# A two-block model on one core: router slots from a threshold, conditioning blocks moved into the conformer, and five smaller edits

## The chip, the cores and the metric

One core of a Trainium2 chip runs the whole forward pass in one launch. The metric is the device time of one execution in microseconds; lower is better. TensorE does the matmuls (PE in the profile, its weight loads PEld), VectorE is DVE, ScalarE ACT, GpSimd POOL, SyncE SP. SP, ACT and POOL also issue DMAs.

## The reference

The input is 512 tokens of width 1024 in float32. A first block mixes tokens (an RWKV-7 mixer in both directions beside a gated linear attention, GLA) and then runs a mixture of 32 experts. A second block has two layers: layer 0 mixes with RG-LRU and Hyena filters, layer 1 with a conformer convolution, and after each stands a mixture of 16 experts in which every expert picks its tokens:

```python
def _adaln(cvec, w_mod, b_mod, n_chunks):
    m = jax.nn.silu(cvec) @ w_mod[:, :n_chunks * D_MODEL] + b_mod[:n_chunks * D_MODEL]
    return [m[:, None, j * D_MODEL:(j + 1) * D_MODEL] for j in range(n_chunks)]

def _ec_moe(h, router, w1, w3, w2):
    cap = EC_CAPACITY * n // N_EXPERTS_2                     # 64 tokens for each expert
    probs = jax.nn.softmax(jnp.einsum('bnd,de->ben', h, router).astype(jnp.float32), axis=1)
    gates, idx = lax.top_k(probs, cap)
    xs = h[bidx, idx]
    a = jnp.einsum('becd,edf->becf', xs, w1)
    g = jnp.einsum('becd,edf->becf', xs, w3)
    y = jnp.einsum('becf,efd->becd', jax.nn.silu(a) * g, w2) * gates[..., None].astype(h.dtype)
    return jnp.zeros_like(h).at[bidx, idx].add(y)

# each layer l of the second block, x of 512 tokens
sh1, sc1, g1, sh2, sc2, g2 = _adaln(c, w_mod[l], b_mod[l], N_MOD)    # N_MOD = 6
xl = xl + g1 * mixer(_modulate(_rmsnorm(xl, norm1_g[l]), sh1, sc1))
xl = xl + g2 * _ec_moe(_modulate(_rmsnorm(xl, norm2_g[l]), sh2, sc2), ...)
```

The kernel takes the softmax over the experts for each token, and the order of tokens within an expert doesn't matter to the sum.

## The kernel before

The program is one stream of instructions for each engine. A framework takes the Python program, gives tiles their memory and lets its scheduler order the instructions of every engine by its own estimate of their times, earlier lines of the program first where several are ready; on the chip each engine then follows its fixed order and waits where something is late. A tile with `bufs=n` rotates over n buffers.

`phase1` (L238) normalises the input (L305 to L316: squares, one root for the four token tiles, a scaling by ScalarE, transposes into `hT`), runs four `rwkv_pair`s and the GLA, and fills in twelve conditioning blocks: `adaln_block(l, j)` (L899) streams 8 tiles of 512 KB of `w_mod` through two buffers and multiplies them by the conditioning vector, four column groups at a time (L905, L907); j = 0, 1, 3, 4 give shifts and scales in `mods`, j = 2 and 5 give gates that go through memory. `mixed` (L616) writes the mixer's output by a DMA on SP.

`residual` (L787) multiplies by the output projection, and `norm_tile` (L857) transposes each token tile, multiplies it by the router, takes the root of the mean square and writes the normalised rows to `xrow`. `moe1` (L1518) runs 16 pairs of the first 32 experts; the output rows of the first 15 go to memory (`yslot`) and are gathered back for each token (L1672, L1673), those of the last pair are added by a matmul (L1690) with a gate matrix `ohT` that is made before it (L1675 to L1683).

`moe2` (L1838) is the experts of the second block. From the router's logits it makes the softmax (L1871 to L1876), transposes it to 16 experts by 512 tokens, finds the 64th largest value of each expert by eight rounds of MAX8 (L1886, L1888), then counts and scans along the tokens to number the slots (L1891 to L1899) and transposes back to `R` (L1902, L1904). `experts` (L1774) prepares each pair of experts: a one-hot matrix `oh` (L1783, for two pairs at a time), a matmul that reads token indices from it (L1789), a gather of the rows (L1711), transposes to `xT` (L1716) and a transposed one-hot `ohT` (L1798). `ffn` does up and gate (L1493) and down (L1513) from a ring of weight tiles of 1 MB (`ring`, L1447), and `outputs` scales and adds (L1750 to L1761).

`mixer1` (L1345) is the conformer: for each of eight feature tiles two products (`product`, L1199, 24 matmuls each, weights split into two parts by ScalarE and VectorE), then 14 convolution taps on VectorE (L1378) and running sums; after the loop the statistics (L1363).

Of the kernel before, what the change touches and what calls it, by code (L numbers as in the profile page):

```python
# [20 lines left out]
T, D = 512, 1024  # L21
NT, KT = 4, 8
# [157 lines left out]
class Kern:  # L180
# [57 lines left out]
    def phase1(self, _):  # L238
# [4 lines left out]
        with ExitStack() as es:  # L243
# [61 lines left out]
            for t in range(NT):  # L305
                nc.scalar.activation(S("bk", D), xs[t], AF.Square, accum_out=rs[:, t:t + 1])
            nc.scalar.activation(rs, rs, AF.Sqrt, scale=1.0 / D, bias=self.eps)
            V.reciprocal(rs, rs)
            for t in range(NT):
                nc.scalar.activation(xs[t], xs[t], AF.Copy, scale=rs[:, t:t + 1])  # L310
                for b in range(2):
                    ps = bank("mm").rearrange("p (a b) -> p a b", a=4)
                    for k in range(4):
                        nc.tensor.transpose(ps[:, k], xs[t][:, (4 * b + k) * 128:(4 * b + k + 1) * 128], ident)
                    V.tensor_mul(hT[:, 4 * b:4 * b + 4, 128 * t:128 * t + 128], ps,
                                 c("ln1_w", 4 * b, 4)[:, :, None].to_broadcast([128, 4, 128]))  # L316
# [9 lines left out]
            def shifted(ft, out):  # L326
# [16 lines left out]
                     for l in range(2) for j in range(6))  # L343
# [5 lines left out]
            fill(6)  # L349
# [5 lines left out]
            fill(3)  # L355
            gl(99)
            fill(99)
# [499 lines left out]
    def norm_tile(self, M, W, bank, t, wr, ps_):  # L857
        nc, V = self.nc, self.nc.vector
        x = self.xres[:, t]
        xn = M.xn[t]  # L860
        rs = M.rs[:, t:t + 1]
        xT = W([128, KT, 128], "xTt", bufs=2)
        for b in range(2):
            ps = bank(("gat", "cb")[b], 1).rearrange("p (k n) -> p k n", k=4)
            for k in range(4):
                nc.tensor.transpose(ps[:, k], x[:, 512 * b + 128 * k:512 * b + 128 * k + 128], self.ident)
            (V.tensor_copy if b else nc.scalar.copy)(xT[:, 4 * b:4 * b + 4], ps)
        for k in range(KT):
# [476 lines left out]
    def mixer1(self, ey):  # L1345
# [3 lines left out]
        with ExitStack() as es:  # L1349
# [8 lines left out]
            us, acc = [], []  # L1358

# [6 lines left out]
            for i in range(KT):  # L1366
# [151 lines left out]
    def moe1(self, yT):  # L1518
        nc, tc, A = self.nc, self.tc, self.A
        with ExitStack() as es:  # L1520
# [138 lines left out]
            for pair in range(15):  # L1659
                if pair % 2 == 0 and pair < 14:  # L1660
                    tokens(pair // 2 + 1)
                z = slice(128 * pair, 128 * pair + 128)
                xT = self.rows_load(P, bank, tok[:, pair:pair + 1], 128) if pair else xT0
                self.rows_ffn(P, bank, xT, self.yslot[z], self.take, 2)
# [3 lines left out]
            for t in range(NT):  # L1668
                for j, g in enumerate((w1, e2)):
# [4 lines left out]

            oh = P([128, D], "yo", bufs=2)[:, 0:512].rearrange("p (t e s) -> p t e s", t=NT, e=2)  # L1675
            V.tensor_tensor(oh, R[:, :, 30:32, None].to_broadcast([128, NT, 2, 64]),
                            self.iota[:, None, None, 0:64].to_broadcast([128, NT, 2, 64]), op=OP.is_equal)
            V.tensor_mul(oh, oh, gl[:, :, :, None].to_broadcast([128, NT, 2, 64]))
            ps = bank("tr", 1)
            for t in range(NT):  # L1680
                nc.tensor.transpose(ps[:, 128 * t:128 * t + 128], oh[:, t].rearrange("p e s -> p (e s)"), self.ident)
            ohT = P([128, KT, 128], "xT", bufs=2).rearrange("p k n -> p (k n)")[:, 0:T]
            nc.scalar.copy(ohT, ps)  # L1683
# [52 lines left out]
    def outputs(self, P, bank, ys, g, m, g2, ohT, last=False):  # L1736
# [5 lines left out]
        def parts(n):  # L1742
            a, b = (P([128, 512], t, F32R, bufs=2 if last and n else self.nbuf)
                    for t in (("h", "h") if last and n and self.nbuf == 1 else ("yhi", "ylo")))
# [3 lines left out]
            else:  # L1748
                y = P([128, 512], "y32")
# [24 lines left out]
    def experts(self, P, bank, R, gt, affine, ne, ff, g2):  # L1774
# [4 lines left out]
        def prepare(pair):  # L1779

            if pair % 2 == 0:
                oh = self.oh = P([128, NT, 4, 64], "oh", F32R)
                V.tensor_tensor(oh, R[:, :, 2 * pair:2 * pair + 4, None].to_broadcast([128, NT, 4, 64]),  # L1783
                                self.iota[:, None, None, 0:64].to_broadcast([128, NT, 4, 64]), op=OP.is_equal)
            oh = self.oh[:, :, 2 * (pair % 2):2 * (pair % 2) + 2]
# [52 lines left out]
    def moe2(self, l, yT):  # L1838
        nc, tc, A, V = self.nc, self.tc, self.A, self.nc.vector
        with ExitStack() as es:  # L1840
# [24 lines left out]
            self.ring_more(M, (ring, "w", 7 + l, 7 + l))  # L1865
# [15 lines left out]
            q, wk, gt, eq = (P([128, T], n, **k)[:16] for n, k in (("hT", dict(bufs=2)), ("y32", {}), ("h", dict(bufs=2)), ("h", dict(bufs=2))))  # L1881
            nc.scalar.copy(q, ps[:16])
            V.tensor_copy(wk, q)
            m8 = P([16, 8], "m8")
            for r in range(8):
                V.max(out=m8, in_=wk)  # L1886
                if r < 7:
                    V.match_replace(out=wk, in_to_replace=m8, in_values=wk, imm_value=-1.0)  # L1888
            cnt = P([16, 1], "c16")
            one = self.ones[:16, 0:1].to_broadcast([16, T])  # L1890
            V.tensor_scalar(gt, q, m8[:, 7:8], 0.0, op0=OP.is_gt, op1=OP.add, accum_out=cnt)  # L1891
            V.tensor_scalar(cnt, cnt, -1.0, 64.0, op0=OP.mult, op1=OP.add)
            V.tensor_scalar(eq, q, m8[:, 7:8], None, op0=OP.is_equal)
            V.tensor_tensor_scan(wk, one, eq, 0.0, OP.mult, OP.add)
            V.scalar_tensor_tensor(eq, wk, cnt, eq, op0=OP.is_le, op1=OP.mult)
            V.tensor_add(gt, gt, eq)
            V.tensor_tensor_scan(wk, one, gt, 0.0, OP.mult, OP.add)
            V.tensor_mul(wk, wk, gt)
            V.tensor_scalar(wk, wk, -1.0, None, op0=OP.add)  # L1899
            ps = bank("tr", 1)[:, 0:64].rearrange("p (t n) -> p t n", t=NT)  # L1900
            for t in range(NT):
                nc.tensor.matmul(ps[:, t], wk[:, 128 * t:128 * t + 128], self.ident[:16, 0:16], start=True, stop=True)  # L1902
            R = P([128, NT, 16], "R")
            V.tensor_copy(R, ps)  # L1904
# [3 lines left out]
            V.scalar_tensor_tensor(gt[:, :, :, 0], R, 0.0, p, op0=OP.is_ge, op1=OP.mult)  # L1908
# [120 lines left out]
```

## Time and profile before

| | us |
|---|---|
| median of 3 runs (lowest, highest) | 2886.4 (2882.2, 2889.4) |
| the profiled execution | 2891.0 |
| its span, first to last instruction | 2889.4 |
| TensorE busy in the span | 2454.6 |
| VectorE busy | 1124.1 |
| ScalarE busy | 643.5 |
| moved by DMA | 778.4 MB, mean 269 GB/s |

Times in the trace are microseconds from the span's start. The stages follow each other: `phase1` to 606, the first experts to 1303, the mixer of layer 0 to 1560, its residual to 1606, its experts to 2136, the conformer to 2288, its residual to 2346, the last experts to 2870, the final norm to 2889. A matmul of float32 shows as two instructions, a transpose as one.

### The profile page before, as it was taken

The page shows a single profiled execution, that of the slowest core. Times are in us where ns is not written, and L with a number is a line of the kernel's source. Part 1 is how long each engine was busy: PE and PEld are TensorE (multiplying, and loading weights), DVE is VectorE, ACT ScalarE, POOL GpSimd, SP SyncE. Part 2 cuts the span into 40 slices and gives each one's busy share as a digit, 9 for nine tenths or more (in the row PEclk, how much of TensorE's full clock was granted, in tenths as well). Part 3 has the DMA queues.
Part 4 walks back from the last instruction along what each step waited for, and adds up shares of the span by engine and source line. Part 5 has one row for each costly group of instructions (what it writes and reads, how often), then busy time and mean ns, then how long its engine had stood idle before and what let it go on. Part 6 is the DMA issues. An engine that isn't in the chain of part 4 may idle for free. (4 is left out here: it accounts for less than half of the span.)

```text
span 2889.4 us, 36529 instructions
## 1 busy us (share of the span) xinstructions
PE 2454.6 (85%) x15158; PEld 1352.8 (47%) x15158; DVE 1124.1 (39%) x2143; ACT 643.5 (22%) x1049; POOL 107.0 (4%) x193
## 2 busy tenths in 40 slices
PE   7999998775999988868889688988989669888897
PEld 3565655663534544436567433333347553333343
DVE  3867767534121320015875411111239641211112
ACT  3223313221102430005721200010034321000001
POOL 1000000001110000010000000000000000000000
PEclk9999998776999999988899798999999779999999
DMA  4355343056998999983133599999954259999996
GB/s 150 121 174 171 108 129 124 18 187 251 396 367 328 397 393 398 396 346 124 59 124 135 208 409 386 392 406 405 409 195 132 104 203 362 399 405 405 400 409 252
DMA packets 244551, 778.42 MB, mean 269 GB/s; under 512 B 15963, under 2 KB 17243, under 8 KB 243488
## 3 DMA queue, kind: packets, MB, share of 16 engines
q1 hardware_dynamic: 223616, 711.77, 65.2%
q0 software_dynamic: 12448, 41.50, 3.7%
q10 hardware_dynamic: 8320, 22.80, 2.2%
q8 instruction: 120, 1.97, 0.3%
q14 instruction: 47, 0.39, 0.0%
HBM read 748.73 MB, written 27.28 MB: 269 GB/s over the span
## 5 line engine op out<-in xcount | busy, mean ns | idle before, releaser
L1493 PE MATMUL G<-w,xT 128*64 128x256 f32 (+1 forms) x4096 | 772.4, 507 | 22.5 <-DMA w<-in_moe_w_up_dram 18.1
L1493 PEld LDWEIGHTS G<-w,xT 128*64 128x64 f32 x4096 | 293.1, 140 | 380.2 <-issue 287.6
L1513 PE MATMUL Y<-w,hT 128*64 128x512 f32 x1536 | 402.7, 602 | 2.6 <-DMA w<-in_moe_w_down_dram 1.3
L1513 PEld LDWEIGHTS Y<-w,hT 128*64 128x64 f32 x1536 | 172.2, 137 | 195.3 <-issue 182.6
L1498 DVE TENSOR_TENSOR h<-h,G 128x256 f32<-128x256 f32 (+1 forms) x64 | 35.4, 553 | 516.8 <-PE G L1493 406.8
L1761 DVE TENSOR_TENSOR xres<-xres,cb 128x512 f32<-128x512 f32 x116 | 79.6, 687 | 115.4 <-PE cb L1759 115.4
L1750 DVE SCALAR_TENSOR_TENSOR y<-Y,gate,g 128x512 f32<-128x512 f32 x32 | 24.0, 751 | 233.9 <-PE Y L1513 232.3
L321 PE MATMUL mm<-hT,w 128*128 128x512 f32 x240 | 113.2, 611 | 0.0
L1716 PE MATMUL gat<-ident,xg 128*128 128x128 f32 x128 | 30.4, 371 | 95.4 <-DMA xg<-xrow,tok 95.3
L1497 ACT ACTIVATE h<-G 128x256 f32<-128x256 f32 (+1 forms) x64 | 31.4, 491 | 343.3 <-PE G L1493 337.6
L1504 ACT COPY hT<-tr 128x256 f32<-128x256 f32 (+1 forms) x64 | 30.7, 479 | 274.8 <-PE tr L1503 274.8
L907 PE MATMUL ad<-wm,sc 128*32 128x256 f32 x768 | 70.5, 410 | 20.5 <-DMA wm<-in_w_mod_dram 19.1
L1209 PE MATMUL b<-big,wh 128*128 128x512 f32 x320 | 84.2, 415 | 4.4 <-ACT wh L854 3.0
L1751 ACT CAST yhi<-y 128x512 fp32r<-128x512 f32 x30 | 18.6, 619 | 310.5 <-DVE y L1750 224.2
L1716 PEld LDWEIGHTS gat<-ident,xg 128*128 128x128 f32 x128 | 19.1, 183 | 117.9 <-DMA xg<-xrow,tok 88.2
L1209 PEld LDWEIGHTS b<-big,wh 128*128 128x128 f32 x320 | 63.0, 199 | 22.6 <-ACT big L1190 5.4
L1759 PEld LDWEIGHTS cb<-yhi,ohT 128*128 128x128 f32 x114 | 21.4, 188 | 105.2 <-DVE xres L1761 56.8
L1503 PE MATMUL tr<-ident,h 128*128 128x128 f32 x192 | 35.8, 297 | 39.1 <-DVE h L1498 39.0
L636 PE MATMUL g<-wb,hT 128*64 128x128 f32 x1024 | 65.5, 276 | 3.3 <-DVE ga L711 2.6
L321 PEld LDWEIGHTS mm<-hT,w 128*128 128x128 f32 x240 | 42.9, 190 | 51.3 <-issue 50.3
L1759 PE MATMUL cb<-yhi,ohT 128*128 128x512 f32 x114 | 57.5, 504 | 9.7 <-ACT yhi L1751 9.7
L1711 POOL DMA_INDIRECT xg<-xrow,tok x32 | 31.1, 972 | 887.6 <-DVE tok L1793 435.7
(677 smaller groups left out, 3564.7 us busy)
## 6 DMA issues: line engine op xcount, KB each, us to landing
w<-in_exp_w_dram SPq DMA_DIRECT2D x384, 1024.0 KB, 13.2
w<-in_moe_w_gate_dram SPq DMA_DIRECT2D x64, 1024.0 KB, 15.6
w<-in_moe_w_up_dram SPq DMA_DIRECT2D x64, 1024.0 KB, 15.0
w<-in_moe_w_down_dram SPq DMA_DIRECT2D x64, 1024.0 KB, 15.3
wm<-in_w_mod_dram SPq DMA_DIRECT2D x96, 512.0 KB, 4.2
ws<-in_w_in_dram SPq DMA_DIRECT2D x20, 512.0 KB, 4.1
ws<-in_cf_w_dram SPq DMA_DIRECT2D x20, 512.0 KB, 3.5
st<-in_w_out_dram SPq DMA_DIRECT2D x16, 512.0 KB, 4.1
```

The lines of the kernel that those rows point to most:

```text
L321: nc.tensor.matmul(ps[:m], w[:, k, col0:col0 + m], hT[:, k], start=k == 0, stop=k == KT - 1)
L636: nc.tensor.matmul(ps[half[h], b], hT[:, k, 64 * j:64 * j + 64], w[h][:, k], start=k == 0, stop=k == KT - 1)
L907: nc.tensor.matmul(ps[32 * g:32 * g + 32, 0:256], self.sc[:, k], w[:, 256 * g:256 * g + 256], start=k == 0, stop=k == KT - 1, tile_positio ...
L1209: nc.tensor.matmul(ps, a[:, k], b[:, k], start=m == 0 and k == 0, stop=m == 2 and k == KT - 1)
L1493: nc.tensor.matmul(parts[m][64 * c:64 * c + 64], xT[:, k, 64 * e:64 * e + 64], w[:, kk, H * c:H * c + H], start=k == 0, stop=k == KT - 1)
L1497: nc.scalar.activation(h, parts[0], AF.Silu)
L1498: nc.vector.tensor_mul(h, h, parts[1])
L1503: nc.tensor.transpose(ps[:, j].rearrange("p c s -> p (c s)"), h[:, 128 * j:128 * j + 128], self.ident)
L1513: nc.tensor.matmul(ys[n][64 * e:64 * e + 64], hTs[e][:, f], ws[e][:, ff_, 512 * n:512 * n + 512], start=f == 0, stop=f == nf - 1)
L1716: nc.tensor.transpose(ps[:, k], xg[:, 512 * b + 128 * k:512 * b + 128 * k + 128], self.ident[:m, :m])
L1759: nc.tensor.matmul(ps, ohT[:m, 128 * t:128 * t + 128], p[k][:m], start=k == 0, stop=k == 1)
L1761: V.tensor_add(xr, xr, ps)
```

## The change

- **Norm of phase 1**: the root is taken for each token tile alone; instead of scaling the tile on ScalarE, VectorE makes a diagonal matrix `dg` of the scales (one buffer), and the transposes become matmuls with it.
- **Conditioning**: `phase1` does eight of the twelve blocks, (0, 0) to (0, 5), (1, 0) and (1, 1). The conformer does (1, 2) to (1, 5), one behind each of its feature tiles 1 to 4, with two buffers for `w_mod` tiles, and sets up the conditioning vector anew.
- **`mixed`** issues its DMA on ScalarE's queue.
- **`norm_tile`**: the root goes to a tile `sd` of its own; for the last token tile an Exp of it, whose result nobody reads, follows.
- **Gate matrix of the first experts**: `ohT` is made during pair 2, in the buffer that held `lnrow`.
- **Later experts**: MAX8 reads the transposed softmax from PSUM; the 64th value goes back to all partitions by a matmul, tokens above and equal to it are counted by matmuls in bf16, and the slots follow by operations with tokens on the partitions. `oh` is made for each pair alone. Some buffers change places, and the ring has one tile more (18 in both layers instead of 17).

```diff
-            nc.scalar.activation(rs, rs, AF.Sqrt, scale=1.0 / D, bias=self.eps)
-            V.reciprocal(rs, rs)
-            for t in range(NT):
-                nc.scalar.activation(xs[t], xs[t], AF.Copy, scale=rs[:, t:t + 1])
+                r = rs[:, t:t + 1]
+                nc.scalar.activation(S("bk", D), xs[t], AF.Square, accum_out=r)
+                nc.scalar.activation(r, r, AF.Sqrt, scale=1.0 / D, bias=self.eps)
+                V.reciprocal(r, r)
+                dg = P([128, 128], "nwr")
+                V.tensor_scalar(dg, ident, r, None, op0=OP.mult)
...
-                        nc.tensor.transpose(ps[:, k], xs[t][:, (4 * b + k) * 128:(4 * b + k + 1) * 128], ident)
+                        nc.tensor.matmul(ps[:, k], xs[t][:, (4 * b + k) * 128:(4 * b + k + 1) * 128], dg, start=True, stop=True)
...
-                     for l in range(2) for j in range(6))
+                     for l, j in ((0, 0), (0, 1), (0, 2), (0, 3), (0, 4), (0, 5), (1, 0), (1, 1)))
...
-            fill(6)
+            fill(4)
...
-            fill(3)
+            fill(2)
             gl(99)
-            fill(99)
...
-        self.nc.sync.dma_start(self.ymix[k], o)
+        self.nc.scalar.dma_start(self.ymix[k], o)
...
-        nc.scalar.activation(rs, rs, AF.Sqrt, scale=1.0 / D, bias=self.eps)
-        V.reciprocal(rs, rs)
+        sd = M.P([128, 2], "sd")
+        nc.scalar.activation(sd[:, 0:1], rs, AF.Sqrt, scale=1.0 / D, bias=self.eps)
+        V.reciprocal(rs, sd[:, 0:1])
+        if t == NT - 1:
+            nc.scalar.activation(sd[:, 1:2], sd[:, 0:1], AF.Exp)
...
+            self.adaln_setup(P)
...
+                if 0 < i < 5:
+                    self.adaln_block(1, i + 1, lambda: H([128, D], "junk", bufs=2), bank, lambda: P([128, T], "t2", bufs=4)[:, 0:256])
...
+                if pair == 2:
+                    lnrow = M.P([128, D], "lnrow")
+                    oh = lnrow[:, 0:512].rearrange("p (t e s) -> p t e s", t=NT, e=2)
...
+                    ohT = lnrow[:, 512:1024]
+                    nc.scalar.copy(ohT, ps)
...
-            self.ring_more(M, (ring, "w", 7 + l, 7 + l))
+            self.ring_more(M, (ring, "w", 8 + l, 8 + l))
...
+            dg, ps = P([16, 16], "dg"), bank("bg", 1)[:, 0:16]
+            V.tensor_scalar(dg, self.ident[:16, 0:16], m8[:, 7:8], None, op0=OP.mult)
+            nc.tensor.matmul(ps, self.ones[:16], dg, start=True, stop=True)
+            th = P([128, 16], "th")
+            V.tensor_copy(th, ps)
+            m = P([128, NT, 2, 16], "gq", BF16)
+            t3 = th[:, None].to_broadcast([128, NT, 16])
+            V.tensor_tensor(m[:, :, 0], p, t3, op=OP.is_gt)
+            V.tensor_tensor(m[:, :, 1], p, t3, op=OP.is_equal)
+            ps = bank("tr", 1)[:, 0:160].rearrange("p (t a n) -> p t a n", t=5, a=2)
+            for t in (4, 0, 1, 2, 3):
+                for s_ in range(t):
+                    nc.tensor.matmul(ps[:, t], self.onesb, m[:, s_], start=s_ == 0, stop=t == 4 and s_ == 3)
+                if t < 4:
+                    nc.tensor.matmul(ps[:, t], self.beforeb, m[:, t], start=t == 0, stop=True)
+            need, pos = P([128, 16], "need"), ps[:, 0:4]
+            V.tensor_scalar(need, ps[:, 4, 0], -1.0, 64.0, op0=OP.mult, op1=OP.add)
+            n3 = need[:, None].to_broadcast([128, NT, 16])
+            R, eq = P([128, NT, 16], "R"), P([128, NT, 16], "eq")
+            V.tensor_tensor(eq, pos[:, :, 1], n3, op=OP.is_lt)
+            V.tensor_mul(eq, eq, m[:, :, 1])
+            V.tensor_add(eq, eq, m[:, :, 0])
+            V.tensor_tensor(R, pos[:, :, 1], n3, op=OP.min)
+            V.tensor_add(R, R, pos[:, :, 0])
+            V.scalar_tensor_tensor(R, R, 1.0, eq, op0=OP.add, op1=OP.mult)
+            V.tensor_scalar(R, R, -1.0, None, op0=OP.add)
```

## Rows read from the trace of the kernel before

**Rows 1.** Stretches: us, each engine's busy us (instructions), TensorE clock, DMA share, GB/s.
```profile
40.00:480.00 440.00, 414.75 (x4643) 257.59 (x4643) 311.58 (x622) 132.04 (x224) 14.60 (x30) 0.97 0.41 132
480.00:606.00 126.00, 87.89 (x1312) 71.80 (x1308) 66.16 (x163) 32.25 (x51) 1.95 (x4) 0.74 0.14 48
...
1649.00:2136.00 487.00, 439.04 (x1887) 173.30 (x1886) 84.17 (x147) 44.77 (x90) 5.68 (x6) 0.95 0.97 384
...
2161.00:2223.00 62.00, 61.82 (x273) 51.19 (x274) 53.07 (x90) 24.75 (x29) 0.00 (x0) 1.00 0.31 98
```
**Rows 2.** Waits, 1649 to 2140 (TensorE), 1560 to 2121 (SP's queue): total, times, longest.
```profile
PE gat L1716 <- DMA xg<-xrow,tok: 27.8, 6, 5.7
...
SPq L1447 <- PE G L1493: 294.7, 114, 30.7
```
**Rows 3.** Timeline in phase 1: start, duration, engine, operation, [idle before, releaser].
```profile
198.60 0.64 PE L907 MATMUL ad<-wm,sc 128*32 128x256 f32 x8 [0.77 <-DMA wm<-in_w_mod_dram]
```
**Rows 4.** The tile wm: who waited for it, us in total, times.
```profile
  PE ad L907: 19.1, 19
```
**Rows 5.** Stretch 40 to 480, instructions of line 907 alone.
```profile
40.00:480.00 440.00, 59.03 (x672) 16.01 (x672) 0.97 0.41 132
```
**Rows 6.** Timeline of the conformer, TensorE and VectorE.
```profile
2228.67 3.78 PE L1209 MATMUL b<-hh,wh 128*128 128x512 f32 x8 [5.08 <-ACT wh L854]
...
2267.86 3.57 PE L1363 MATMUL s<-ones,sum 128*128 128x1 f32 x16 [14.43 <-DVE sum L1388]
...
2259.83 7.25 DVE L1378 SCALAR_TENSOR_TENSOR cy<-ug,pc,cy 128x64 f32<-128x64 f32 x14 [1.44 <-ACT cy L1374]
```
**Rows 7.** Timeline of the router of layer 0, up to the gathered rows.
```profile
1612.94 1.28 ACT L1873 ACT_TABLE_LOAD   x1
...
1617.21 0.57 ACT L1882 COPY hT<-tr 16x512 f32<-16x512 f32 x1 [2.72 <-PE tr L1880]
...
1618.27 0.68 DVE L1886 MAX8 m<-y 16x8 f32<-16x512 f32 x1
...
1629.43 0.73 DVE L1891 TENSOR_SCALAR_CACHE_REDUCE h<-hT,m 16x512 f32<-16x512 f32 x1
...
1638.01 0.25 DVE L1908 SCALAR_TENSOR_TENSOR gt<-R,prob 128x64 f32<-128x64 f32 x1
1638.15 1.22 DVE L1783 TENSOR_TENSOR oh<-R,iota 128x1024 fp32r<-128x1024 f32 x1
...
1642.04 1.01 POOL L1711 DMA_INDIRECT xg<-xrow,tok  x1 [28.29 <-DVE tok L1793]
...
1646.77 1.12 PE L1716 MATMUL gat<-ident,xg 128*128 128x128 f32 x4 [0.62 <-DMA xg<-xrow,tok]
```
**Rows 8.** Timeline of the first router: its counts in bf16.
```profile
682.04 0.27 PE L1598 MATMUL gat<-ab,onesb 128*128 128x32 bf16 x4
```
**Rows 9.** The chain that ended last, a gather late in the last layer: start, us.
```profile
2715.96 8.27 DMA xg<-xrow,tok
```
**Rows 10.** Timeline of the first experts' end, TensorE and ScalarE's queue.
```profile
1288.09 1.09 PE L1681 MATMUL tr<-ident,yo 128*128 128x128 f32 x4 [11.38 <-DVE yo L1678]
...
1295.63 7.67 PE L1513 MATMUL Y<-w,hT 128*64 128x512 f32 x32
...
1303.33 0.36 ACTq L1213 DMA_DIRECT2D eo<-in_ln_f_w_dram  x1
```
**Rows 11.** The tile w, 1255 to 1320: issues (ns min/median/max, first and last start), landings.
```profile
L1447 SPq DMA_DIRECT2D w<-in_moe_w_down_dram x4: 2473/3393/3702, 1261.0 to 1270.8; - x4
...
DMA to landing us min/median/max: 21.8/22.5/22.8
```
**Rows 12.** Timelines in phase 1: scaling, transposes, two-pass matmuls of 128x128.
```profile
15.94 4.27 ACT L310 ACTIVATE ar<-ar,rs 128x1024 f32<-128x1024 f32 x4 [0.24 <-DVE rs L308]
...
23.88 1.10 PE L314 MATMUL mm<-ident,ar 128*128 128x128 f32 x8
...
207.44 1.16 PE L462 MATMUL sc<-ident,bk 128*128 128x128 f32 x8
```

More of the change, by code (lines that the diff above doesn't have):

```diff
@@ L305, in phase1 @@
             for t in range(NT):
-                nc.scalar.activation(S("bk", D), xs[t], AF.Square, accum_out=rs[:, t:t + 1])
-            nc.scalar.activation(rs, rs, AF.Sqrt, scale=1.0 / D, bias=self.eps)
-            V.reciprocal(rs, rs)
-            for t in range(NT):
-                nc.scalar.activation(xs[t], xs[t], AF.Copy, scale=rs[:, t:t + 1])
+                r = rs[:, t:t + 1]
[4 more added lines that the diff above has]
+                V.tensor_scalar(dg, ident, r, None, op0=OP.mult)
                 for b in range(2):
@@ L1661, in moe1 @@
                     tokens(pair // 2 + 1)
+                if pair == 2:
+                    lnrow = M.P([128, D], "lnrow")
+                    oh = lnrow[:, 0:512].rearrange("p (t e s) -> p t e s", t=NT, e=2)
+                    V.tensor_tensor(oh, R[:, :, 30:32, None].to_broadcast([128, NT, 2, 64]),
+                                    self.iota[:, None, None, 0:64].to_broadcast([128, NT, 2, 64]), op=OP.is_equal)
+                    V.tensor_mul(oh, oh, gl[:, :, :, None].to_broadcast([128, NT, 2, 64]))
+                    ps = bank("tr", 1)
+                    for t in range(NT):
+                        nc.tensor.transpose(ps[:, 128 * t:128 * t + 128], oh[:, t].rearrange("p e s -> p (e s)"), self.ident)
+                    ohT = lnrow[:, 512:1024]
+                    nc.scalar.copy(ohT, ps)
                 z = slice(128 * pair, 128 * pair + 128)
@@ L1673, in moe1 @@
                     V.scalar_tensor_tensor(self.xres[:, t], y, g[:, t:t + 1], self.xres[:, t], op0=OP.mult, op1=OP.add)
[L1675 to L1683, printed above, removed]
             o = self.rows_ffn(P, bank, xT, None, self.take, 2)
@@ L1743, in parts @@
             a, b = (P([128, 512], t, F32R, bufs=2 if last and n else self.nbuf)
-                    for t in (("h", "h") if last and n and self.nbuf == 1 else ("yhi", "ylo")))
+                    for t in (("hT", "hT") if last and n and self.nbuf == 1 else ("yhi", "ylo")))
             if g2 is None:
@@ L1748, in parts @@
             else:
-                y = P([128, 512], "y32")
+                y = P([128, 512], "h", bufs=2)
                 V.scalar_tensor_tensor(y[:m], ys[n][:m], g[:m], g2[:m, 512 * n:512 * n + 512], op0=OP.mult, op1=OP.mult)
@@ L1779, in prepare @@
         def prepare(pair):
[L1781 to L1785, printed above, removed]
+            oh = P([128, NT, 2, 64], "oh", F32R)
+            V.tensor_tensor(oh, R[:, :, 2 * pair:2 * pair + 2, None].to_broadcast([128, NT, 2, 64]),
+                            self.iota[:, None, None, 0:64].to_broadcast([128, NT, 2, 64]), op=OP.is_equal)
             ps = bank("bg", 1)
@@ L1880, in moe2 @@
                 nc.tensor.matmul(ps[:16, 128 * t:128 * t + 128], p[:, t], self.ident, start=True, stop=True)
[L1881 to L1884, printed above, removed]
+            wk, m8 = P([128, T], "hT", bufs=2)[:16], P([16, 8], "m8")
             for r in range(8):
-                V.max(out=m8, in_=wk)
+                q = wk if r else ps[:16]
+                V.max(out=m8, in_=q)
@@ L1887, in moe2 @@
                 if r < 7:
[L1888 to L1902, printed above, removed]
@@ L1903, in moe2 @@
-            R = P([128, NT, 16], "R")
-            V.tensor_copy(R, ps)
+                    V.match_replace(out=wk, in_to_replace=m8, in_values=q, imm_value=-1.0)
+            dg, ps = P([16, 16], "dg"), bank("bg", 1)[:, 0:16]
[4 more added lines that the diff above has]
+            m = P([128, NT, 2, 16], "gq", BF16)
@@ L1906, in moe2 @@
+            V.scalar_tensor_tensor(R, R, 1.0, eq, op0=OP.add, op1=OP.mult)
+            V.tensor_scalar(R, R, -1.0, None, op0=OP.add)
             gt = P([128, NT, 16, 3], "gt")
             V.tensor_copy(gt[:, :, :, 1:3], self.tokid[:, :, None].to_broadcast([128, NT, 16, 2]))
-            V.scalar_tensor_tensor(gt[:, :, :, 0], R, 0.0, p, op0=OP.is_ge, op1=OP.mult)
+            V.tensor_mul(gt[:, :, :, 0], p, eq)
             self.experts(P, bank, R, gt, affine, 16, 1024, g2)
```

## The prediction

> **What bounds the kernel now.** I read the stages first, then who waits in each, then the rows around every edit. The profiled execution took 2891.0 us (span 2889.4 and 1.6 around it), 4.6 above the median of 2886.4 of the runs; the sum below is made on the profile and then taken off the median.
>
> By stages [rows 1]: in the first mixer, from 40 to 480, TensorE is busy 414.75 of 440 us, VectorE 311.58. So TensorE's throughput sets the pace there; the tail from 480 to 606 is a chain of short steps (TensorE 87.89 of 126 at a clock of 0.74). In the first expert layer of the second block (1649 to 2136) TensorE is busy 439.04 of 487, and DMA carries 384 GB/s. Both look full, so the waits decide: TensorE's longest wait in that stretch is for gathered rows (27.8 us in six), no wait for a weight is listed at all, and it is the loads' queue that waits for TensorE to free slots, 294.7 us [rows 2]. Weights are not late; TensorE is the bound, and what counts is when its first matmul can start. The other expert layer of that block repeats this. In the conformer's product loop (2161 to 2223) TensorE is busy 61.82 of 62 us and VectorE 53.07 [rows 1]: TensorE is full, VectorE close behind.
>
> **Part by part.** *Adaln blocks out of phase 1.* One weight tile of a block costs TensorE 8 matmuls in 0.64 us, a block of 8 tiles 5.1, four blocks 20.5 [rows 3]. Waits for w_mod tiles cost 19.1 us over twelve blocks, so four carry 6.4 more: 26.9 us at most [rows 4]. Of the 12 x 64 matmuls 672 lie between 40 and 480 [rows 5]; the other 96, 1.5 blocks, lie before that or in the tail, where TensorE has gaps, and I count them at nothing. That leaves 2.5 blocks of 6.7, or 16.8 us, of throughput. A sixth of it I give back, since with less matmul work the mixer's own chains will show their waits: -14, bounds -27 and 0. The 32 w_mod loads go from SP too, and with them what they held up there.
>
> *The same four blocks in the conformer.* They sit between products in a loop where TensorE is full. They bring 20.5 us of matmuls and, at phase 1's mean, 6.4 of waits. Hidden are three things [rows 6]. TensorE stands 5.08 us for a weight tile at 2228.67. After that pause it runs at the lower clock (8 matmuls in 3.78 us, the usual time being nearer 2): about 3 us. And it waits 14.43 us for the sums at 2267.86, while VectorE's last slice needs 7.25 for its taps and, as I estimate it, some 3.5 around them: 3.5 us of slack. 26.9 - 5.1 - 3 - 3.5 gives +15. Behind the waiting matmuls stand the next products on TensorE, and behind the w_mod loads, which wait for one of two buffers, the product weights on SP. If each tile waits as in the densest stretch of phase 1 (0.77 us at 198.60 [rows 3], on half of the 32 tiles, 12 us) and nothing is hidden, it is 20.5 + 12, or +33; if the blocks fall into the pauses, +3.
>
> *Slots of the later experts* (twice). Up to the one-hot matrix `oh`, the chain of the router loses three things [rows 7]. The Exp table load ahead of the softmax (1.28) moves to where ScalarE idles. The two copies before the first MAX8 go, from 1617.21 to 1618.27 (1.06). And the scans: from 1629.43 to the end of `oh` (1638.15 + 1.22) are 9.94 us. In their place come a tiny matmul with an operation before and one after it, some 0.8 us; two comparisons and eight operations on at most 128x64, 0.25 each as L1908, 2.5; 14 bf16 count matmuls, where four took 0.27 [rows 8], under 1; half of `oh`, 0.6; and hand-overs, about 0.5. That is 5.4, so 4.5 less. Together the token index is 6.8 us earlier. What is late next is the gather: issued at 1642.04, it was used at 1646.77, 4.7 us later [rows 7]; 6.8 us earlier it runs beside weight loads, as the gather that took 8.27 [rows 9]. So the first expert matmul comes 3.3 to 6.8 earlier; I take 5.5, since the ring is nearly filled by then. Twice: -11, bounds -7 and -14.
>
> *One more weight buffer.* Nothing waits for weights [rows 2]: 0. Were DMA the bound, one load of 1.05 MB at 384 GB/s would be worth 2.7 us in each layer, -5; a fuller queue could lengthen the gathers, whose mean wait is 4.6 us in six cases: at most +2.
>
> *Gate matrix early.* At the end of the first experts, TensorE stands 11.38 us at 1288.09 behind the transposes of `oh`, for VectorE; the last pair's matmuls are queued behind them, and its Y ends 7.67 us after 1295.63 [rows 10]. With `oh` long done, the last w_down tile is late next: issued up to 1270.8, landing 22.5 us on, at 1293.3 [rows 11]. The quarter of Y that needs it ends near 1297 to 1300: 3 to 6 us earlier. But the matrix now lies in the `lnrow` buffer until the last add, some 7 us past Y, and the next mixer's first buffer `eo` starts its load at 1303.33, right when Y ends, so it seems to wait for that memory. If it must now wait for the adds, nothing is left, or +3. I take -1, bounds -5 and +3. The early work (two operations, four transposes, one copy) hides under pair 2.
>
> *Norm at the start.* Four scalings by ScalarE (4.27 us [rows 12]) go; 32 transposes become matmuls with a diagonal. Eight transposes took 1.10 us, four two-pass matmuls of that size 1.16 [rows 12], so each tile pays about 1.1 more, and the one diagonal buffer makes tiles wait for each other. Tile 0 starts earlier, the last tile hardly: -1, bounds -4 and +3. The Trainium skill ("TensorE: Matmul & The Clock Gate", Terms) says that the transpose mode is four times faster for FP32; by that factor the 32 matmuls would cost about 13 us more instead of 4, which no row bears out, as the two-pass form stands at twice.
>
> *The output of the mixer on ScalarE's queue*: eight issues of about 0.36 (as L1213's [rows 10]) move past SP, where they held back weight loads; on ScalarE the next copy waits behind each. 0, bounds -3 and +3. The Trainium skill ("Trainium Kernel Development and Optimization", Key Constraints) says that issuing from several engines saves only the sequencer's issue time; that agrees with 0.
>
> The sum: -14 + 15 - 11 + 0 - 1 - 1 + 0 = -12 us: 2879 for the profiled execution, 2874 for the median, 0.4% less.
>
> **The rivals.** *The conformer pays back more than phase 1 gains* (ends slower). Place: TensorE between products. For it: 61.82 of 62 us busy. Against it: the pauses at 2228 and 2267. Price: +33, phase 1 giving only 7 because its own chains take over; with -11 and -2 that is +13, or 2899. It decides where the blocks cost the conformer over 29 us against 7.
>
> *The blocks fill pauses*: phase 1 gives 27, the conformer takes 3, the routers 13: with -2 it is -39, 2847. For it: the waits for w_mod tiles, 19.1 us, are most of what TensorE idles between 40 and 480, 25 us; against it: the full stretch of the conformer.
>
> *It cancels*: the moved blocks cost 22 and gain 14, the gathers eat the routers' gain down to -7, the rest is 0: +1, so 2887. For it: the 8.27 us gather and TensorE as the bound on both sides of the move. That the threshold and the buffer do nothing belongs here.
>
> *Transposes at a quarter of the matmul's price* (the page's factor, as a mechanism of this kernel): 13 instead of 4 us at the start, +9, 2883; the row of L462 speaks against it.
>
> **How the numbers follow.** Forecast 0.44 (about 2860 to 2877); the payback 0.17; the pauses filled 0.13; cancelled 0.23; the quarter price 0.03. What a measurement of this kernel can tell from no change is about 0.3%, 8.7 us. Faster: 0.44 + 0.13 = 0.57; within: 0.23 + 0.03 = 0.26; slower: 0.17. The range from 2850 to 2897 leaves out about half of the two outer cases and takes in the bounds of the small parts.
>
> **What would show it.** The expert layers' first matmuls 3 to 7 us sooner after the residual's last; no waits for weights there, as before; the gap of 11.38 us gone and `eo`'s load later than Y's end; phase 1's end near 590; the conformer from the experts' last add to the residual's first matmul 12 to 18 us longer, with waits for w_mod tiles between products. Wrong would be: a conformer no longer than before, a phase 1 that ends as before, or an order of instructions, set by the framework's scheduler over the whole program, that moves work nobody edited: a few us each way that I can't see from here.

## The result, and the profile after

The changed kernel takes 2918.9 us (median of 4 runs, 2913.9 to 2924.5) where the kernel before, run beside it, takes 2886.6: 1.1% slower, ratio 1.0114, 95% interval 1.0092 to 1.0136. The profiled execution has a span of 2917.0 us against 2889.4. I had forecast 2874, faster. One of the twelve executions of e9 below took 6816.9 us and is left out of its time and its ratio.

The first table cuts both traces at the same landmarks: the residual's first and last matmul, the first matmul of the experts' G, the end of their last Y.

| stage, us | before | after | difference |
|---|---|---|---|
| start to the first residual (first mixer) | 614.1 | 595.2 | -18.9 |
| residual and first router | 101.1 | 99.4 | -1.7 |
| first experts | 588.1 | 581.6 | -6.5 |
| second mixer, to its residual | 247.2 | 254.6 | +7.4 |
| its residual | 55.9 | 55.9 | 0 |
| router, later layer 0 | 42.9 | 37.8 | -5.1 |
| experts, later layer 0 | 486.2 | 481.8 | -4.4 |
| conformer, to its residual | 152.5 | 213.1 | **+60.6** |
| its residual | 56.3 | 56.4 | 0 |
| router, later layer 1 | 41.8 | 38.7 | -3.1 |
| experts, later layer 1 | 483.3 | 485.6 | +2.3 |
| end | 19.9 | 16.9 | -3.0 |

One stage loses 60.6 us; all others together gain 33. Its stretches, in the columns of [rows 1]; the first three lines answer to the first three there:

```profile
40.00:480.00 440.00, 409.80 (x4582) 261.75 (x4580) 317.53 (x653) 139.21 (x233) 8.77 (x18) 0.96 0.33 105
480.00:586.00 106.00, 70.81 (x1106) 61.06 (x1106) 54.84 (x122) 24.25 (x40) 0.00 (x0) 0.73 0.02 6
...
1626.00:2106.00 480.00, 435.65 (x1876) 171.89 (x1873) 83.81 (x146) 43.85 (x87) 5.67 (x6) 0.96 0.98 387
...
2106.30:2319.40 213.10, 149.03 (x737) 100.33 (x737) 131.63 (x225) 69.35 (x95) 8.88 (x20) 0.79 0.42 139
...
2152.00:2170.00 18.00, 15.56 (x96) 9.51 (x96) 12.82 (x23) 3.97 (x5) 0.92 (x2) 1.00 0.76 249
2170.00:2224.00 54.00, 30.01 (x180) 14.95 (x180) 20.44 (x38) 6.05 (x8) 2.90 (x7) 0.63 0.57 182
```

The same cut of the kernel before, conformer only:

```profile
2135.50:2288.10 152.60, 110.60 (x474) 88.45 (x473) 126.23 (x213) 68.42 (x91) 0.80 (x2) 0.88 0.26 83
```

TensorE is busy 38.4 us longer and idle 22.1 us longer. From 2170 to 2224 it is busy only 30 of 54 us, where [rows 1] had 61.82 of 62, and its mean granted clock there is 0.63: mostly the lower of its two levels (1.2 of 2.4 GHz). By groups in the conformer, after (busy us, mean ns | idle before, releaser):

```profile
L1214 PE MATMUL b<-hh,wh 128*128 128x512 f32 x128 | 43.4, 480 | 5.5 <-ACT wh L855 4.5 <-ACT hh L1195 0.5
L1214 PE MATMUL b<-hl,wh 128*128 128x512 f32 x128 | 36.9, 430 | 0.0
L1214 PE MATMUL b<-hh,wl 128*128 128x512 f32 x128 | 33.3, 398 | 0.0
L912 PE MATMUL b<-junk,sc 128*32 128x256 f32 x256 | 25.4, 489 | 28.7 <-DMA junk<-in_w_mod_dram 28.6
...
L928 PE MATMUL b<-sel,t 128*128 128x8 f32 x8 | 2.0, 363 | 1.1 <-ACT t L925 1.1
```

and before:

```profile
L1209 PE MATMUL b<-hh,wh 128*128 128x512 f32 x128 | 35.5, 414 | 8.8 <-ACT wh L854 5.1 <-ACT hh L1190 3.5
L1209 PE MATMUL b<-hl,wh 128*128 128x512 f32 x128 | 32.7, 399 | 0.0
L1209 PE MATMUL b<-hh,wl 128*128 128x512 f32 x128 | 31.6, 389 | 0.0
```

So the 60.6 us are: the blocks' own matmuls, 27.4; the products, which are the same 384 but 13.8 us slower (113.6 against 99.8); waits for w_mod tiles (`junk`), 28.6; less about 8 us of old waits that became shorter: for the products' inputs `hh` (3.5 to 0.5), for the sums (14.4 to 9.8) and, by 0.6 only, for product weights. (These add to 62; modelled ends overlap a little.) Not all of the 13.8 is owed to waits for tiles. In e1 (below), which has no block in the conformer, the products take 103.1 us, 3.3 more than before, since the first one runs at the lower clock there as it does here (14 matmuls in 8.3 us in both, with the waits for `hh` nearly gone); its first group:

```profile
L1215 PE MATMUL b<-hh,wh 128*128 128x512 f32 x128 | 38.4, 439 | 6.4 <-ACT wh L856 5.3 <-ACT hh L1196 0.5
```

And some 2.5 us are a slower pace at the higher clock, which the last section shows. About 8 are left, and 5.5 of them lie in the two products behind the second and third block, at the lower clock. The timeline of TensorE shows how this looks, first where products are left to put between tiles, then where none is:

```profile
2155.30 0.64 PE L912 MATMUL b<-junk,sc 128*32 128x256 f32 x8
2155.87 0.97 PE L1214 MATMUL b<-hl,wh 128*128 128x512 f32 x3
...
2157.23 0.64 PE L912 MATMUL b<-junk,sc 128*32 128x256 f32 x8
...
2171.58 1.08 PE L912 MATMUL b<-junk,sc 128*32 128x256 f32 x8 [3.43 <-DMA junk<-in_w_mod_dram]
2172.84 1.08 PE L912 MATMUL b<-junk,sc 128*32 128x256 f32 x8 [0.18 <-DMA junk<-in_w_mod_dram]
2176.80 1.08 PE L912 MATMUL b<-junk,sc 128*32 128x256 f32 x8 [2.88 <-DMA junk<-in_w_mod_dram]
2178.70 1.08 PE L912 MATMUL b<-junk,sc 128*32 128x256 f32 x8 [0.82 <-DMA junk<-in_w_mod_dram]
...
2191.81 3.76 PE L1214 MATMUL b<-hh,wh 128*128 128x512 f32 x8
2195.37 3.04 PE L1214 MATMUL b<-hl,wh 128*128 128x512 f32 x8
2198.25 2.02 PE L1214 MATMUL b<-hh,wl 128*128 128x512 f32 x8
```

In the second part a pair of tiles comes every 5 us; no product stands between the tiles of blocks 2 and 3, while blocks 1 and 4 got some. The landings of `junk`, after (min, median, max):

```profile
DMA to landing us min/median/max: 3.8/4.7/6.9
```

Two buffers and 4.7 us to land are one tile in 2.35 us, of which TensorE needs 0.64. After 20 us of this, eight matmuls of a product take 3.76 us instead of 2.02: the lower clock.

### The profile page after: what moved, and what is told of

It is laid out like the page before. It is cut to its first block, busy times and chain, and to the rows that moved or that the text cites. A ratio compares the mean times of both kernels' runs of the same rounds, so it can differ in the third digit from the quotient of the medians.

```text
span 2917.0 us, 36650 instructions
## 1 busy us (share of the span) xinstructions
PE 2477.7 (85%) x15206; PEld 1364.9 (47%) x15206; DVE 1117.5 (38%) x2159; ACT 638.7 (22%) x1051; POOL 107.7 (4%) x195
## 3 DMA queue, kind: packets, MB, share of 16 engines
q8 instruction: 121, 1.98, 0.3%
## 5 line engine op out<-in xcount | busy, mean ns | idle before, releaser
L1761 DVE SCALAR_TENSOR_TENSOR h<-Y,gate,g 128x512 f32<-128x512 f32 x32 | 24.0, 751 | 211.7 <-PE Y L1522 209.9
L1762 ACT CAST yhi<-h 128x512 fp32r<-128x512 f32 x30 | 18.6, 619 | 297.9 <-DVE h L1761 203.8
L1512 PEld LDWEIGHTS tr<-ident,h 128*128 128x128 f32 x192 | 21.5, 148 | 102.8 <-DVE h L1507 97.6
L637 PEld LDWEIGHTS g<-wb,hT 128*64 128x64 f32 x1024 | 60.2, 142 | 14.1 <-issue 4.8
L323 PEld LDWEIGHTS mm<-hT,w 128*128 128x128 f32 x240 | 42.9, 190 | 50.7 <-issue 50.2
L856 DVE TENSOR_TENSOR wl<-ws,wh 128x1024 fp32r<-128x1024 f32 x36 | 44.0, 1223 | 56.6 <-PE b L1214 56.0
```

The costliest lines, as they stand in the source:

```text
L323: nc.tensor.matmul(ps[:m], w[:, k, col0:col0 + m], hT[:, k], start=k == 0, stop=k == KT - 1)
L637: nc.tensor.matmul(ps[half[h], b], hT[:, k, 64 * j:64 * j + 64], w[h][:, k], start=k == 0, stop=k == KT - 1)
L856: self.nc.vector.tensor_sub(lo, x, hi.bitcast(F32))
L1512: nc.tensor.transpose(ps[:, j].rearrange("p c s -> p (c s)"), h[:, 128 * j:128 * j + 128], self.ident)
```

## The experiments

Conformer and first mixer are measured between the landmarks of the table. Ratios are to the kernel before, run beside each.

| run | time, us | ratio (95%) | first mixer | conformer |
|---|---|---|---|---|
| after | 2918.9 | 1.0114 (1.0092 to 1.0136) | 595.2 | 213.1 |
| e1 blocks back | 2879.3 | 0.9983 (0.9970 to 0.9995) | 621.8 | 152.4 |
| e2 blocks alone | 2938.0 | 1.0187 (1.0172 to 1.0202) | 592.2 | 214.0 |
| e3 four tiles | 2899.4 | 1.0047 (1.0032 to 1.0061) | 599.4 | 189.3 |
| e4 one tile loaded | 2889.3 | 1.0014 (1.0003 to 1.0026) | 601.2 | 181.9 |
| e5 dealt out | 2881.9 | 0.9993 (0.9981 to 1.0006) | 600.0 | 176.9 |
| e6 dealt out, rest early | 2884.7 | 1.0006 (0.9992 to 1.0020) | 593.9 | 181.1 |
| e7 e1 and old norm | 2880.5 | 0.9994 (0.9977 to 1.0010) | 621.1 | 152.3 |
| e8 e1 and output on SP | 2876.3 | 0.9959 (0.9943 to 0.9976) | 611.9 | 153.2 |
| e9 dealt out, rest late | 2880.7 | 0.9988 (0.9973 to 1.0003) | 604.0 | 169.7 |
| e10 after, output on SP | 2922.4 | 1.0136 (1.0117 to 1.0155) | 604.7 | 212.2 |
| e11 = e8 again | 2880.3 | 0.9983 (0.9970 to 0.9995) | 616.9 | 153.1 |

**Is it the blocks?** e1 undoes their move and nothing else (below); e2 is the kernel before with their move and nothing else.

```
-                if 0 < i < 5:
-                    self.adaln_block(1, i + 1, ...)
...
+                     for l in range(2) for j in range(6))
```

> The changed kernel, with all twelve blocks of the adaptive norm back in the first mixer as before; every other edit stays. Theory (the four blocks in the conformer carry the loss): the conformer, from the end of the first later experts' Y to the residual's first matmul, goes from 214.0 us back to 152.6 +- 4, the first mixer's end comes 10 to 19 us later, and the time is 2918.9 - 61.4 + 10 to 19, so 2867 to 2877: under the kernel before. Rival (the order that the scheduler chose, not the blocks): the conformer stays over 180 us and the time over 2895.

> The kernel before, with only the four blocks moved to the conformer (two more stay in the first mixer's last fills). Theory (the move costs by itself): the conformer takes 205 to 220 us in place of 152.6, the first mixer ends 14 to 19 us sooner, the time is 2886.6 + 61 - 17 = 2931, 2922 to 2938. Rival (the move is dear only together with the other edits): 2880 to 2905.

The conformer falls to 152.4 in e1 and stands at 214.0 in e2. The blocks carry the loss, by themselves and in either company. e1's time is 2 us over its range; its first mixer ended 26.6 us later than in the changed kernel, not 10 to 19. e2's ended 21.9 us sooner than before, not 14 to 19. How much the move costs in all is less certain: 1.3% between e1 and the changed kernel, 1.9% in e2, whose three other executions took 8 to 11 us more than the profiled one (2928.9), in stages that no profile shows.

**Which part of it: the wait for tiles, or TensorE's work?** e3 (first) gives the tiles four places, two of them in the one tile `cyall` that now holds all eight outputs of the convolution (J is `junk` with its two buffers); e4 (second) loads one of eight tiles.

```
+            cy = P([128, KT, T], "cyall")
+            cv = [cy[:, q:q + 2].rearrange("p k t -> p (k t)") for q in (4, 6)]
...
+            wm = itertools.cycle((J, lambda: cv[0], J, lambda: cv[1]))
...
-                    self.adaln_block(1, i + 1, lambda: H([128, D], "junk", bufs=2), ...)
+                    self.adaln_block(1, i + 1, lambda: next(wm)(), ...)
```

```
-            w = w4()
-            nc.sync.dma_start(w, ...)
+            if k == 0 or l == 0 or j < 2:
+                w = w4()
+                nc.sync.dma_start(w, ...)
```

> The changed kernel, with four places for w_mod tiles in the conformer instead of two (the two new ones lie in the memory of convolution outputs that are not written yet; the last block has three). Theory (two buffers against a load of 4.7 us: a tile can come every 2.35 us at best where a block's eight tiles stand together, and needs 0.64 of TensorE): a tile can come every 1.2 us, TensorE's waits for w_mod tiles fall from 28.6 to under 12 us, the stretch at the lower clock shrinks with them, the conformer takes 180 to 195 us, the time is 2885 to 2900. Rival (the queue of SP or the rate of the transfers sets the pace): waits over 22 us, the conformer over 205, the time over 2910.

> The changed kernel, where each of the four blocks in the conformer loads one w_mod tile and its eight steps all read that one: seven of eight loads left out, all matmuls kept, so layer 1's scale, shift and gates are other numbers than the reference's. Theory (waiting for tiles and the lower clock behind the waits): both go, the blocks cost the matmuls alone, 20 to 26 us less the pauses they fill, the conformer takes 165 to 180 us, the time is 2870 to 2887. Rival (TensorE's own work for the blocks, at whatever clock): the conformer stays over 200 us and the time over 2905.

Groups of e3, then of e4, in the conformer:

```profile
L912 PE MATMUL b<-junk,sc 128*32 128x256 f32 x144 | 12.5, 427 | 7.4 <-DMA junk<-in_w_mod_dram 7.2
L912 PE MATMUL b<-cyall,sc 128*32 128x256 f32 x112 | 9.7, 420 | 1.9 <-DMA cyall<-in_w_mod_dram 1.9
```

```profile
L1215 PE MATMUL b<-hh,wh 128*128 128x512 f32 x128 | 41.1, 461 | 2.2 <-ACT wh L855 1.2 <-ACT hh L1196 0.5
...
L913 PE MATMUL b<-junk,sc 128*32 128x256 f32 x256 | 14.6, 380 | 0.0
L929 PE MATMUL b<-sel,t 128*128 128x8 f32 x8 | 2.0, 363 | 13.3 <-ACT t L926 13.3
```

e3: with the same queue and the same transfers the waits for tiles fall from 28.6 to 9.1 us and the conformer by 23.8. So the queue and the rate of transfers were not what held the tiles up; the number of buffers against the landing time was. e4: without waits for tiles the conformer is still 29.4 us longer than before, a little over my range. Its 14.6 us of matmuls explain half. Another wait stands where the first one was: the transposing matmul of a block needs a copy from ScalarE. ScalarE and VectorE in e4, at the second block:

```profile
2173.94 7.25 DVE L1385 SCALAR_TENSOR_TENSOR cy<-ug,pc,cy 128x64 f32<-128x64 f32 x14
...
2181.28 0.63 ACT L1394 ACTIVATE t<-cy 128x512 f32<-128x512 f32 x1 [7.54 <-DVE cy L1385]
2181.82 0.35 ACT L926 COPY t<-b 128x256 f32<-128x256 f32 x1
```

The copy, 0.35 us long, is queued behind a square that waits 7.5 us for VectorE's taps, and TensorE's next product is queued behind the transposing matmul: 6.6 and 6.7 us, with the lower clock behind each. In the changed kernel the waits for tiles covered this one (1.1 us there).

**Is it where the tiles stand?** e5 to e9 take the block apart and put a few tiles behind each product; the copy gets one product's time before it is used. e6 and e9 leave a rest for TensorE's waits at the end of the loop: e6 ahead of the matmuls of the statistics' rows, e9 behind them (and e9 has the output on SP's queue, below). `adaln_steps` is `adaln_block` with a yield behind each tile and two behind the copy; the last line is e5's, e6 steps by 2 behind the products 3 to 14 and by 6 and the rest around `stats()`, e9 by 2 behind the products 2 to 15 (its expectation says to the fourteenth), by 3 ahead of `stats()`, and takes the rest after the normalisation.

```
+            fill = itertools.chain(*(self.adaln_steps(1, j, ...) for j in (2, 3, 4, 5)))
+            go = lambda n: [next(fill, None) for _ in range(n)]
...
+                for a in (1, 0):
+                    pp.append(self.product(P, bank, A["cf_w1"][8 * a + i], hh, hl))
+                    go(3 if i > 3 else 2)
```

> The changed kernel, with the 32 w_mod tiles of the conformer dealt out two or three behind each product instead of eight behind every second one, and the transposing matmuls of a block one step later than its copy on ScalarE; two buffers as before. Theory (the loss is where the tiles stand, eight together behind a load of two at a time, and the block's wait for ScalarE's copy, with the clock falling behind each pause): both waits go, the matmuls alone are left (32 x 0.57 to 0.64, so 18 to 20 us, less the 5 us pause for a product weight), the conformer takes 165 to 173 us in place of 213, the time is 2871 to 2879. Rival (the matmuls drag VectorE's chain or the weight loads along, wherever they stand): the conformer stays over 180 us, as with one loaded tile (181.9), the time over 2886.

> As the run with the tiles dealt out, but 24 steps behind the products 3 to 14 and the rest behind the last product, where TensorE waits for VectorE's sums and the statistics (12 to 14 us each, twice). Theory: the tiles there are free, since TensorE idles; the conformer takes 160 to 168 us, the time is 2866 to 2874, 0.4 to 0.7% under the kernel before. Rival (the tiles and the block's additions on VectorE delay the statistics): the conformer takes 172 us or more, the time is 2878 or more.

> The dealt-out tiles again (two behind each product from the second to the fourteenth), the last block's rest behind the statistics' last matmuls in program order, and the mixer's output through SP's queue. Theory (what the moved blocks must cost is the matmuls that find no idle TensorE): about 24 tiles stand between products, 24 x 0.55 = 13 us, less the 5 us pause that they fill, the other eight lie in TensorE's waits for VectorE; the conformer takes 160 to 168 us against 152.5, the first mixer ends at 592 to 600, the time is 2862 to 2871, 0.5 to 0.85% under the kernel before. Rival (the blocks push the statistics or the residual back, as with the rest placed ahead of the statistics' rows, 181.1 us): the conformer over 172, the time over 2873, no better than with the blocks back and the output on SP.

Waits of TensorE in the conformer, e5:

```profile
PE s L1378 <- DVE sum L1406: 9.8, 1, 9.8
PE b L915 <- DMA junk<-in_w_mod_dram: 5.0, 6, 1.5
PE b L934 <- ACT t L929: 4.6, 1, 4.6
```

With the same two buffers and the same 32 loads, e5 cuts the conformer by 36 us: where the tiles and the copy stand does more than two more buffers (e3) or seven of eight loads less (e4). It missed its range (165 to 173) by 3.9, about the copy's wait that was left, and its time, 2881.9, missed 2871 to 2879. e6 failed as its rival said. Its last six tiles stood ahead of the rows' matmuls:

```profile
2266.72 1.08 PE L915 MATMUL b<-junk,sc 128*32 128x256 f32 x8 [1.65 <-DMA junk<-in_w_mod_dram]
2267.73 2.08 PE L1429 MATMUL s<-ident,t 128*128 128x128 f32 x8
```

The matmul of L1429 follows the last tile directly, and VectorE's chain to the residual begins with it; in e5 the same stretch, from the sums' matmuls to the rows', took 4.5 us, here 21.4 (L1378 at 2246.34). e9 has them behind it and the conformer at 169.7, near the 168 I had allowed, but the time, 2880.7, is 10 over its range: its first mixer ended at 604.0, not 592 to 600, and a conformer 17 us longer than before spends what the first mixer gains. e9 and e11 differ only in where the four blocks run, and their intervals overlap almost wholly: even better placed, the move is worth nothing that these runs can tell. e9 still waits 11.8 us for tiles; dealt-out tiles with four buffers, which might take that away, were not run.

**The first mixer's other edits.** With the blocks back e1's first mixer seemed 7.7 us longer than before; e7 and e8 undo the norm and the output's queue, one each, on top of e1.

> The run with all blocks back in the first mixer, and there the norm at the start as before too (scalings on ScalarE and transposes). With the blocks back, the first mixer took 621.8 us to the residual's first matmul, 7.7 more than before. Theory (the two-pass matmuls and the order behind them cost that): the first mixer ends at 612 to 617, the time is 2879 - 5 to 9 = 2870 to 2874. Rival (it is the output's DMA on ScalarE's queue): it stays at 619 to 624, the time at 2877 to 2882.

> The run with all blocks back in the first mixer, and the output of the mixer written through SP's queue again. Theory (the output's DMA on ScalarE's queue, each with the next copy behind it, costs the 7.7 us by which the first mixer is longer): it ends at 612 to 617, the time is 2870 to 2874. Rival (the norm at the start, or the order of the scheduler): 619 to 624, the time 2877 to 2882.

e7's first mixer ends at 621.1 and its time is 2880.5: the norm is not what made it longer, and both lie in its rival's ranges. e8 looked like a hit: 611.9, and a time 3 us under e1's, though 2 over its theory's range. So e10 puts only the output back in the changed kernel, and e11 runs e8 a second time.

```
-        self.nc.scalar.dma_start(self.ymix[k], o)
+        self.nc.sync.dma_start(self.ymix[k], o)
```

> The changed kernel, with only the mixer's output back on SP's queue; all else as changed. Theory (the queue of the output matters): the first mixer ends 5 to 10 us sooner than the 593.9 to 601.2 of the four kernels that have it on ScalarE beside the moved blocks, so near 592 or under, and the time falls by 0.15% or more, to 2909 to 2914. Rival (the output costs the same on either queue, and the 8 to 10 us between the profiles with the blocks back are the granted clock, 30.7 and 34.5 us at the lower level before 480 against 17.0): 594 to 601 again, 2915 to 2922.

> The same kernel as the one with the blocks back in the first mixer and the output on SP's queue, a second time beside the two others. If its 0.41% under the kernel before was the edit: 2871 to 2880 again, 0.25 to 0.5% under. If it was the chance of few runs: within 0.25%, as with the output on ScalarE's queue (0.17% under).

e10's first mixer ends at 604.7, later than any that has eight blocks and the output on ScalarE, its time at 2922.4, and e11 has e1's ratio to the digit. The output's queue makes no difference that shows, e8's theory falls, and e8's gain was partly chance. The same kernel twice, e8 and then e11:

```profile
30.00:480.00 450.00, 426.01 (x4708) 262.78 (x4706) 312.95 (x623) 134.44 (x227) 14.61 (x31) 0.98 0.40 130
480.00:605.00 125.00, 85.51 (x1282) 70.00 (x1278) 66.12 (x163) 31.66 (x50) 1.95 (x4) 0.74 0.15 50
```

```profile
30.00:480.00 450.00, 427.26 (x4680) 264.47 (x4680) 313.51 (x627) 133.85 (x227) 14.54 (x30) 0.97 0.40 130
480.00:605.00 125.00, 88.74 (x1299) 72.56 (x1295) 65.60 (x160) 31.53 (x50) 1.94 (x4) 0.72 0.14 48
```

The granted clock is 0.01 and 0.02 lower in e11 and its first mixer 5.0 us longer. One profile of this stage is good to about 5 us, no better. That the clock makes the difference, as e10's rival had it, is not shown: summed over the first 480 us, TensorE is at the lower level for 33.4 us in the changed kernel (595.2) and for 27.4 in e4 (601.2).

**The fastest kernel** of these is the changed one with all blocks left in the first mixer (e1, with the output on either queue): 0.17% under the kernel before in e1 and in e11, 0.41% in e8, each with an interval below 1. It beats both kernels, by little.

## Why the prediction was wrong

*What bounds the kernel* held. No weight is waited for in the later experts; TensorE waits there for gathered rows, as in [rows 2]:

```profile
PE gat L1727 <- DMA xg<-xrow,tok: 26.0, 6, 5.3
```

*Blocks out of the first mixer: -14, bounds -27 and 0.* Right (and the waits of [rows 4] went from 19.1 us to 5.6 in nine between 30 and 620): -18.9 in the two profiles, and 598.8 us as the mean of the eight profiled kernels with eight blocks there (592.2 to 604.7) against 617.2 for the five with twelve (611.9 to 621.8), -18.4. The sixth that I gave back did not show.

*The same blocks in the conformer: +15, bounds +3 and +33.* **This is the step that failed**: +60.6 here, +61.5 in e2. Its upper bound gave half the tiles the 0.77 us wait of [rows 3]. In the sum's own terms: the waits for tiles, put at 6.4, were 28.6; the blocks' matmuls, put at 20.5, took 27.4, thirteen tiles of them at the lower clock (1.08 us for 0.64); the products' slower pace, put at nothing, was 13.8; and the pauses to be filled, put at 11.6 with the clock behind one of them, gave 8. The pause for a product weight did not go (4.45 us, with the lower clock behind it). Why the wait was priced wrong: a wait in the trace is what is left of a delay after the work put in front of it. In the first mixer the tiles come little faster; TensorE has other matmuls between them. Before, from the same stretch as [rows 3], and the landings of `wm`:

```profile
193.04 0.64 PE L907 MATMUL ad<-wm,sc 128*32 128x256 f32 x8 [0.94 <-DMA wm<-in_w_mod_dram]
193.61 2.40 PE L636 MATMUL g<-wb,hT 128*64 128x128 f32 x40
195.95 0.64 PE L907 MATMUL ad<-wm,sc 128*32 128x256 f32 x8
196.52 1.31 PE L636 MATMUL g<-wb,hT 128*64 128x128 f32 x20
...
DMA to landing us min/median/max: 3.5/4.2/6.5
```

One tile in 2.9 us, and the matmuls of L636 fill most of it. A better bound was there to read: the tile wm lands in 4.2 us (median), two buffers make that 2.1 us for a tile, so 32 tiles with nothing between them take 67 us by this estimate, not 20.5 + 12. The tiles themselves took 54 (25.4 + 28.6), since half of them did get products between them. Left out beside it: the clock behind such waits (5.5 us on the products, 0.44 on each of thirteen tiles), and the block's copy on ScalarE, which e4 shows at 13.3 us once the tiles come in time. The rival "the conformer pays back more" named the right stage and sign, but its price came from the same rows: 2899, where 2919 was measured. Its point of decision, 29 us in the conformer, was passed twice over.

*Slots of the later experts: -5.5 each, bounds -3.5 and -7.* Near: -5.1 and -3.1 here; means of the eleven profiled kernels with the edit 37.7 and 38.3 us against 42.9 and 41.8, so -5.2 and -3.5. The gather of layer 0, where the residual ends 19.7 us earlier than before (1606.5 to 1586.7):

```profile
1614.27 1.02 POOL L1722 DMA_INDIRECT xg<-xrow,tok  x1 [20.23 <-DMA w<-in_exp_w_dram]
...
1621.92 1.12 PE L1727 MATMUL gat<-ident,xg 128*128 128x128 f32 x4 [3.36 <-DMA xg<-xrow,tok]
```

Against [rows 7] the gather is issued 27.77 us earlier (1642.04 to 1614.27), of which 19.7 are the stages ahead of it: 8.0 us gained, where I had 6.8. Its rows are used 7.65 us after the issue and not 4.73, so 2.9 go to the gather, which now runs beside the loads (409 GB/s in those 7.7 us, against 113 before): what I had said would be late next.

*One more weight buffer: 0.* Right. Both later expert layers together take 969.5 us before, and 969.5 as the mean of the eleven with it (965.6 to 972.8); single layers move by 5 either way.

*Gate matrix early: -1, with `eo`'s load late.* The sum came out as I had it, and `eo`'s load is late as I had it; the pause did not go. The experts are 6.5 us shorter, but not by the 11.38 us of [rows 10], and it is not the last w_down tile that is late next. TensorE now stands as long ahead of the transposes of h, since h is next in VectorE's queue, behind the same adds of gathered rows (L1694) that `oh` had stood behind:

```profile
1257.41 0.69 PE L1512 MATMUL tr<-ident,h 128*128 128x128 f32 x2 [13.82 <-DVE h L1507]
...
1255.74 1.28 DVE L1694 SCALAR_TENSOR_TENSOR xres<-yo,rt,xres 128x1024 f32<-128x1024 f32 x1 [1.33 <-DMA yo<-yslot,slot]
1256.94 0.41 DVE L1507 TENSOR_TENSOR h<-h,G 128x256 f32<-128x256 f32 x1
```

I had read the releaser of the pause (`yo`, the gate matrix) and not what stood ahead of it in its queue. `eo`'s load, which in [rows 10] was issued as Y ended, waits for the adds, 7.1 us past Y's end (1268.56 + 7.67):

```profile
1268.56 7.67 PE L1522 MATMUL Y<-w,hT 128*64 128x512 f32 x32
...
1283.33 0.35 ACTq L1218 DMA_DIRECT2D eo<-in_ln_f_w_dram  x1
```

The second mixer is 7.4 us longer. Over the eleven the two stages together are 1.8 us shorter (833.5 against 835.3).

*Norm at the start: -1.* e1 against e7 gives +0.7, within what a profile tells. The 64 matmul records with the diagonal take 9.6 us against 6.3 for the 32 transposes, +3.3 where I had counted 4, so the rival at a quarter of the price falls. The Trainium skill ("TensorE: Matmul & The Clock Gate", Terms) gives the transpose mode a factor of four for FP32, by which, as an estimate, it would have been 13 more; the rows decide against it. *Output on ScalarE's queue: 0.* Right, by e10 and e11.

*Not in the sum:* the end is 3.0 us shorter (19.9 to 16.9; 16.5 to 16.9 in all eleven), most likely from the other buffers in `parts`, which no run here separates from the rest. And in e1, where only the small edits are left, they should have been worth -13 and give about -5, while the changed kernel is some 20 us faster than e2, from which the same edits part it; the first mixer's scatter of 5 us a profile is of that order, so which of them is short stays open.

## What to carry to other kernels

A wait that the trace shows for a load is what the work in front of it left of the landing time. Who moves the load's user to another place must price it afresh, as landing time over buffers per tile, with what the new place can put between: here 2.35 us a tile for 0.64 us of work. Moving work between two stages that are both full of the same engine brought nothing that shows here, even spread out (e9 against e11); and behind its long pauses the next matmuls were paid a second time at the lower clock (3.76 us for 2.02).

## What the runs showed of the hardware

Sixty-four block matmuls (as the trace counts them) in one row take 3.66 us in e4, where eight in a row between others take 0.64, so 5.1 for 64: about 0.2 us more for each group of eight that stands alone. That the change of shape costs this is likely but not shown, since the 64 also read one and the same tile.

```profile
2156.97 3.66 PE L913 MATMUL b<-junk,sc 128*32 128x256 f32 x64
```

At the higher clock, a product's eight matmuls take 2.03 us in all eight kernels with blocks in the conformer and 1.98 in the five without, also where no block is near; over 48 such rows that is about 2.5 us. No run says what in the program makes it. From e5, then from e1:

```profile
2139.34 2.03 PE L1220 MATMUL b<-hh,wh 128*128 128x512 f32 x8
...
2166.89 1.98 PE L1215 MATMUL b<-hh,wh 128*128 128x512 f32 x8
```

And the same kernel, the same order, had its first mixer at 611.9 and 616.9 us, and the five that share one order there (after, e3 to e6) had it at 593.9 to 601.2. Between the first two the granted clock differs by 0.01 to 0.02. That is a scatter of several us in one stage, and no effect of an edit.
